# A hybrid diffusion layer on one core: the first norm's modulation as plain float32 products in four column strips, x loaded ahead of it, and three feature tiles that follow h

## The chip, the cores and the metric

The kernel runs on one core of a Trainium2 chip. The metric is device microseconds (us) for one execution of the whole layer; the number given for a kernel is the median of several runs. The engines are named as the profile names them: PE is TensorE (the matmuls, with PEld for its weight loads), DVE is VectorE, ACT is ScalarE, POOL is GpSimd, SP is SyncE, which here only starts DMAs.

## What is computed

One layer runs on 640 tokens: 128 context tokens (with the modulation of `c_ctx`) and 512 latent tokens (with that of `c`). Cut to the part that the change touches, the reference is:

```python
mod = silu(c) @ w_mod + b_mod                      # once for c_ctx, once for c; float32
sh1, sc1, g1, sh2, sc2, g2 = split(mod, 6)
h = rmsnorm(x, ng[0]) * (1.0 + sc1) + sh1          # x: 640 x 1024
z = h @ w_in                                       # zx, zg, q, k, v, g, lr, ga, gb
...                                                # RG-LRU on conv(zx), GLA on q, k, v, two gates, w_out
x = x + g1 * rmsnorm(m, ng[1])
f = square(relu(h2 @ mlp_w1)) @ mlp_w2             # h2: x under the norm with sh2, sc2
x = x + g2 * rmsnorm(f, ng[3])
```

Everything is float32. Products of the kernel reach that accuracy in two ways: plain float32 on PE, or float32r (one pass) on operands that were split into a rounded first part and a remainder, with three passes (first by first, first by remainder, remainder by first).

## The kernel before

**Recorder.** The program is first recorded in an order that is right (class `Recorder`), and then `order` hands every engine its instructions: each engine takes the oldest one whose operands are there by the estimated durations of `cost`. On the chip each engine then works through its list strictly in that order. So a list fixed by estimates decides who stands behind whom.

**Start.** SP loads x in five tiles of 128 tokens, `w_mod` in chunks of 256 columns (1 MB, four transfers of 256 KB, named `modw`), and the weights of the first products (`raw`, 1 MB for two feature tiles). `EARLY` and `MIX` (lines 48 and 49) are strings in which each letter is a step: which loads go first, and in which order the start is recorded. `x_norm` scales x by its inverse norm, `x_T` transposes it on PE into eight feature tiles `xnT`.

**Modulation of the first norm.** Eight chunks: even ones are the scale, odd ones the shift, each for two feature tiles (k tiles) of h. `mod_mm` (line 623) multiplies a chunk with the two conditioning vectors. For chunks 0 and 1 (`MOD_FULL`) it does so in plain float32 (`modw`, `cst`). For the other six it splits the chunk: ACT casts it (`modh`), DVE and POOL in turn subtract (`modl`), and PE takes both parts with the two-part vectors `csh`. The result, a row of 256 values for each request, is copied to SBUF (`rw`) and turned into columns by tiny products with `sel`; DVE makes of them the columns `a1` (scale) and `sh1` (shift).

**h.** `make_h` (line 661) scales and shifts `xnT` (128 columns on DVE, 512 on ACT), DVE casts the result to `HH` and subtracts to `HL`.

**First products.** The first unit (`first_part`, line 808) runs two feature tiles of zx, taking h's eight k tiles as they come. One feature tile is 48 matmuls of 128x320: 8 k tiles, 3 passes, 2 halves of the tokens. All later products (`fm_unit`) are one feature tile at a time, on a PSUM pool `dense` of two tiles; the pool `aux` has two more. After a tile, `post_zx` empties PSUM and does the convolution (copies `zp`, then `cv`, `xc` on ACT and DVE). Weights are split ahead (`whi` on ACT, `wlo` on DVE) into four buffers, `N_W`.

**Background.** After `first_post` (line 814) a long chain of small POOL operations, `softplus_consts` (line 683), makes the constants `n8sp` and `p4sp`. The RG-LRU chains (`xs`, gates `r` and `i`, `th`, scans) need them and run beside the products. Their gate weights `bdr` are loaded after the modulation's chunks, and ACT casts them (`bh`). GLA, the other mixer, and later modulation vectors run in the background too, and the PE goes on with products to the end of the MLP.

The lines below show how a split chunk is multiplied:

```python
copy(MOD_HI[i], hi, raw)                                          # ACT
by[MOD_LO[i]].tensor_tensor(lo, raw, f32(hi), op=OP.subtract)     # DVE or POOL
PE.matmul(out, csh[:, k, :], hi[:, kk, :], start=k == 0, stop=False)
PE.matmul(out[0:2], csh[:, k, 0:2], lo[:, kk, :], start=False, stop=k == KT - 1)
```

Of the kernel before, what the change touches and what calls it, by code (L numbers as in the profile page):

```python
# [12 lines left out]
OP = mybir.AluOpType  # L13
# [21 lines left out]
# w_mod chunks that plain float32 products take; engines (A, V, G) of the parts of the start  # L35
MOD_FULL = (0, 1)
MOD_HI, MOD_LO = "AAAA", "VGVG"
# [7 lines left out]
# the first transfers (x: a token tile, m: 256 columns of w_mod, r: rows of b_mod and norm_g), then the order in which the  # L45
# start is recorded (l: load of w_mod, X: buffers of x^T, x: transposes, m: modulation, h: two k tiles of h, p: split of
# the first weights, d: load of the next)
EARLY = "xxxmxrx"
MIX = "Xlllxlxxxxllmldmpmhmmmmhmhh"


class Op:
    """A recorded instruction."""
# [11 lines left out]
def _runs(ap, f0):  # L65
    """The runs of columns an access touches, [(lo, hi)]."""
# [20 lines left out]
def _meet(a, b):  # L87
    """Whether two accesses of a tile share a byte."""
    if a[0] >= b[1] or b[0] >= a[1]:
        return False  # L90
    ra, rb = a[2], b[2]
    if ra[0][0] >= rb[-1][1] or rb[0][0] >= ra[-1][1]:
        return False
    return any(x < d and c < y for x, y in ra for c, d in rb)
# [6 lines left out]
class Port:  # L101
    """An engine's instructions, recorded instead of issued."""
# [8 lines left out]
class Recorder:  # L111
    """Records the program in an order that is right, then issues it in an order in which no engine
    waits for an operand while another instruction could run: every engine takes the oldest
    instruction whose operands are there by the estimated times. Data hazards and the pools' slots
    (given out in the order of recording) are kept."""
# [18 lines left out]
    def cost(eng, name, args, kw, out):  # L134
        n = _dims(out)
        if eng == "PE":
            if name == "transpose":
                return max(0.05, n * 2 / 2400)
            if args[1].dtype == F32R:
                return max(n / 2400 + 0.0025, 0.106)  # L140
            return max(0.213, n * 4 / 2400)
# [22 lines left out]
    @staticmethod  # L164
    def region(ap):
        """What a hazard is looked for in: a tile of PSUM is a whole, and engines take turns at it."""
        return (0, 128, ((0, 1 << 30),)) if ap.space == bass.MemoryType.PSUM else _region(ap)
# [53 lines left out]
    def order(self):  # L221
# [24 lines left out]
        while len(out) < len(ops):  # L246
# [50 lines left out]
            if e == "PE":  # L297
                # the array runs at half its clock in a window after one that was mostly idle
# [43 lines left out]
class Piece:  # L342
    """One [128, 1024] slice of a weight, split into two float32r parts."""
# [7 lines left out]
class Load:  # L351
    """One transfer of weights into a raw buffer; n pieces are split from it."""
# [6 lines left out]
class Unit:  # L359
    """A run of matmuls on split weights and what follows it."""  # L360
# [7 lines left out]
class Stage:  # L368
    """One step of a chain: its cost (us) on VectorE and ScalarE, what it waits for, slots since the step before."""
# [5 lines left out]
class Chain:  # L375
    """Work that runs beside the large products, one stage after the other."""
# [11 lines left out]
def tile_hybrid_layer(  # L388
# [49 lines left out]
    def scaled(e, dst, src, scale, bias):  # L438
        """dst = src * scale + bias, with one of each to a partition."""
# [5 lines left out]
    # token tile 0 is the prompt; tiles 1..4 are the sample in column-major grid order  # L445
# [21 lines left out]
    # the conditioning vectors first; w_mod's shift and scale columns between the tiles of x  # L467
# [22 lines left out]
    def mod_load(m):  # L490
        """256 columns of the scale (even m) or the shift (odd m) of the first norm, two k tiles to a buffer."""
# [22 lines left out]
    # the array's clock is gated until it has been busy for a while  # L514
# [17 lines left out]
    # silu of the conditioning vectors, [128, k, (ctx, lat)]  # L532
    cst = consts.tile([128, 8, 2], F32, name="cst")
# [7 lines left out]
    # the same in two parts for each request, and what adds a request's parts up  # L541
    csh = consts.tile([128, 8, 4], F32R, name="csh")
    V.tensor_copy(csh[:, :, 0:2], cst)
    V.tensor_tensor(csh[:, :, 2:4], cst, csh[:, :, 0:2].bitcast(F32), op=OP.subtract)
    sel = consts.tile([4, 2], F32, name="sel")
    V.tensor_tensor(sel, ident[0:4, 0:2], ident[0:4, 2:4], op=OP.add)

# [1 line left out]
    w_in_r = w_in[0].rearrange("(k p) n -> p k n", p=128)  # L549

    def fm_pieces(src, n0, ncols):
        """Feature-major pieces of 128 columns, two to a transfer where there are two."""
# [12 lines left out]
    def row_pieces(src, k0):  # L565
        """Token-major pieces: one k tile by 1024 columns, two to a transfer."""
# [33 lines left out]
    junk = consts.tile([128, 512], mybir.dt.bfloat16, name="junk")  # L600

    def rstd_of(ssq, n, scale):
        """(ssq * scale + eps) ** -0.5 in place on [128, n]."""
# [4 lines left out]
    # a = norm_g * (1 + sc), sh: [128, (ctx, lat), k]  # L608
# [14 lines left out]
    def mod_mm(m):  # L623
        """256 columns of the scale (even m) or the shift (odd m) for both requests, as two columns of a1 or sh1."""
        ps = aux()
        out = ps[0:4, 0, 0:256]
        for i, raw in enumerate(modw[m]):
            if m in MOD_FULL:
                for kk in range(2):
                    PE.matmul(out[0:2], cst[:, 2 * i + kk, :], raw[:, kk, :], start=i + kk == 0, stop=2 * i + kk == KT - 1)  # L630
                continue
            hi, lo = (t_(nm, F32R)[:, 0:512].rearrange("p (k n) -> p k n", k=2) for nm in ("modh", "modl"))
            copy(MOD_HI[i], hi, raw)
            by[MOD_LO[i]].tensor_tensor(lo, raw, f32(hi), op=OP.subtract)
            for kk in range(2):
                k = 2 * i + kk
                PE.matmul(out, csh[:, k, :], hi[:, kk, :], start=k == 0, stop=False)
                PE.matmul(out[0:2], csh[:, k, 0:2], lo[:, kk, :], start=False, stop=k == KT - 1)
        rw = t_("rw")
        n = 2 if m in MOD_FULL else 4  # L640
        A.copy(rw[0:n, 0:256], out[0:n])
        for i in range(2):
            k = 2 * (m // 2) + i
            pc = ps[:, 1, 2 * i:2 * i + 2]
            PE.matmul(pc, rw[0:n, 128 * i:128 * (i + 1)], sel[0:n], start=True, stop=True)
            if m % 2:
                V.tensor_scalar(cols["sh1"][:, :, k], pc, bm(0, k), None, op0=OP.add)
            else:
                V.tensor_scalar(cols["a1"][:, :, k], pc, bm1[:, k:k + 1], ng(0, k), op0=OP.add, op1=OP.mult)
# [18 lines left out]
    # the gates' weights of two heads, [(copy, in), head, direction, (gate, out)]  # L668
# [9 lines left out]
    # softplus(-L), exactly: max(-L, 0) + 2 atanh(y / (2 + y)), y = exp(-|L|)  # L678
# [25 lines left out]
    def startup():  # L704
        do_loads(1)
# [11 lines left out]
        for s_ in MIX:  # L717
            if s_ == "l":
                modw.append(mod_load(len(modw)))
            elif s_ == "m":  # L720
                mod_mm(nm)
# [9 lines left out]
            elif s_ == "d":  # L731
                do_loads()
# [952 lines left out]
```

## Time and profile before

| what | value |
|---|---|
| three runs | 1179.06, 1180.85, 1172.89 us (median 1179.06) |
| profiled execution, span from the first to the last instruction | 1176.6 us |
| mean granted PE clock | 0.992 |
| PE busy in the span | 1146.1 us (97%) |
| DVE, ACT, POOL busy | 773.2, 571.5, 99.6 us |
| HBM read | 117.94 MB |

The profile is of one execution. Its own total is not listed apart from its span; the median of the runs lies 2.5 us above that span, which is what start and end around the first and last instruction would take if it was a median run. In the profile, a row of a timeline is one or several like instructions of an engine, with the start, the time until the last of them ended, the operation, the tile written and the tiles read, the shapes and the count; the bracket behind it is the engine's idle time just before and what released it. All helpers record through one line (L339), so tiles tell the steps apart. A plain float32 matmul stands in the trace as two records, a float32r one as one. The time to landing of a DMA counts from its issue.

### The profile page before, as it was taken

How to read it: one execution, taken by the hardware profiler on the slowest of the kernel's cores; microseconds unless marked ns; L12 is line 12 of the kernel's file. 1: busy time of each engine (PE TensorE's matmuls, PEld its weight loads, DVE VectorE, ACT ScalarE, POOL GpSimd, SP SyncE). 2: the span in 40 equal slices, each digit the busy share in tenths (PEclk: the TensorE clock that was granted, in tenths of full speed). 3: DMA queues.
4: the chain of work that ended last, by engine and by line, in shares of the span. 5: the costliest groups of instructions: out<-in, count | busy, mean ns of one | idle time of the engine just before them, and what ended most of it. 6: DMA issues, size and time to landing. Idle time of an engine off the chain costs nothing.

```text
span 1176.6 us, 17840 instructions
## 1 busy us (share of the span) xinstructions
PE 1146.1 (97%) x7188; PEld 1071.5 (91%) x7188; DVE 773.2 (66%) x1159; ACT 571.5 (49%) x911; POOL 99.6 (8%) x163
## 2 busy tenths in 40 slices
PE   7799899999999999999999999999999999999996
PEld 5599899999999999999999879999999999988995
DVE  4977966778484737629977478986455544555546
ACT  6668897995574758512342278422222222222222
POOL 3646113000000000000000021000000000000001
PEclk9999999999999999999999999999999999999998
DMA  9625336341312212227543446632322222222202
GB/s 279 217 63 153 110 84 172 77 129 55 108 59 68 72 55 72 90 89 240 174 169 134 145 139 198 214 121 72 104 76 72 72 72 72 72 73 81 94 5 89
DMA packets 101011, 130.65 MB, mean 111 GB/s; under 512 B 7790, under 2 KB 77632, under 8 KB 100928
## 3 DMA queue, kind: packets, MB, share of 16 engines
q1 hardware_dynamic: 98880, 127.61, 34.9%
q0 software_dynamic: 2048, 1.90, 0.6%
q8 instruction: 56, 0.92, 0.3%
q14 instruction: 27, 0.22, 0.1%
HBM read 117.94 MB, written 3.68 MB: 103 GB/s over the span
## 4 chain that ended last, share of the span: by engine, by line
PE 76%; DVE 8%; DMA 6%; ACT 4%; issue 3%; POOL 2%; SPq 0%; DVEq 0%; POOLq 0%; ACTq 0%
PE dense L339 62%; PE aux L339 15%; DMA modw<-in_w_mod_dram 2%; DVE i L339 2%; DMA i<-r 1%; DVE wlo L339 1%; DMA r<-r 1%; DMA raw<-in_w_in_dram 1%; DVE th L339 1%; DMA xb<-in_x_sample_dram 1%; POOL spp L339 1%; ACT r L339 1%; ACT th L339 1%; ACT whi L339 1%; DVE cv L339 1%
## 5 line engine op out<-in xcount | busy, mean ns | idle before, releaser
L339 ACT CAST whi<-raw 128x1024 fp32r<-128x1024 f32 (+1 forms) x159 | 164.2, 1037 | 392.8 <-PE dense L339 365.6
L339 DVE TENSOR_TENSOR wlo<-raw,whi 128x1024 fp32r<-128x1024 f32 x154 | 188.0, 1223 | 170.7 <-ACT whi L339 170.2
L339 PE MATMUL dense<-HH,whi 128*128 128x320 f32 x784 | 182.1, 313 | 5.6 <-DVE lrs L339 3.6
L339 PE MATMUL dense<-HL,whi 128*128 128x320 f32 x784 | 180.5, 311 | 0.6 <-DVE HL L339 0.6
L339 PE MATMUL dense<-HH,wlo 128*128 128x320 f32 x768 | 176.9, 311 | 0.0
L339 PEld LDWEIGHTS dense<-HH,whi 128*128 128x128 f32 x784 | 131.7, 189 | 7.0 <-DVE lrs L339 3.9
L339 PEld LDWEIGHTS dense<-HL,whi 128*128 128x128 f32 x784 | 132.1, 189 | 0.9 <-DVE HL L339 0.7
L339 PEld LDWEIGHTS dense<-HH,wlo 128*128 128x128 f32 x768 | 129.5, 189 | 0.2
L339 PE MATMUL dense<-H2H,whi 128*128 128x320 f32 (+2 forms) x496 | 116.8, 309 | 0.0
L339 PE MATMUL dense<-H2H,wlo 128*128 128x320 f32 (+2 forms) x496 | 116.5, 308 | 0.0
L339 PE MATMUL dense<-H2L,whi 128*128 128x320 f32 (+2 forms) x496 | 116.5, 308 | 0.0
L339 PEld LDWEIGHTS dense<-H2H,whi 128*128 128x128 f32 x496 | 84.6, 188 | 1.2
L339 PEld LDWEIGHTS dense<-H2L,whi 128*128 128x128 f32 x496 | 84.0, 188 | 0.0
L339 PEld LDWEIGHTS dense<-H2H,wlo 128*128 128x128 f32 x496 | 83.9, 188 | 0.0
L339 DVE SCALAR_TENSOR_TENSOR mac<-mw,cst,mac 128x512 f32<-128x512 f32 x112 | 77.9, 749 | 2.7 <-DMA mw<-in_w_mod_dram 2.5
L339 PE MATMUL dense<-whi,al 128*128 128x512 f32 (+1 forms) x192 | 75.2, 392 | 0.0
L339 PE MATMUL dense<-wlo,ah 128*128 128x512 f32 (+1 forms) x192 | 75.2, 392 | 0.0
L339 PE MATMUL dense<-whi,ah 128*128 128x512 f32 (+1 forms) x192 | 75.1, 391 | 0.0
L339 PE MATMUL aux<-whi,al 128*128 128x512 f32 (+1 forms) x132 | 51.6, 391 | 0.0
L339 PE MATMUL aux<-wlo,ah 128*128 128x512 f32 (+1 forms) x132 | 51.6, 391 | 0.0
L339 PE MATMUL aux<-whi,ah 128*128 128x512 f32 (+1 forms) x132 | 51.5, 390 | 0.0
L339 ACT ACT_TABLE_LOAD x36 | 46.2, 1283 | 2.5 <-DMA r<-r 1.1
(310 smaller groups left out, 2235.6 us busy)
## 6 DMA issues: line engine op xcount, KB each, us to landing
raw<-in_mlp_w_dram SPq DMA_DIRECT2D x34, 1024.0 KB, 5.4
raw<-in_w_in_dram SPq DMA_DIRECT2D x24, 1024.0 KB, 5.3
mw<-in_w_mod_dram SPq DMA_DIRECT2D x64, 256.0 KB, 5.9
modw<-in_w_mod_dram SPq DMA_DIRECT2D x32, 256.0 KB, 5.9
raw<-in_w_out_dram SPq DMA_DIRECT2D x8, 1024.0 KB, 4.9
i<-r SPq DMA_DIRECT2D x32, 160.0 KB, 3.4
raw<-in_w_in_dram SPq DMA_DIRECT2D x8, 512.0 KB, 4.3
raw<-in_lru_up_dram SPq DMA_DIRECT2D x4, 1024.0 KB, 5.3
```

The source lines that it names most:

```text
L339: getattr(eng[o.eng], o.name)(*o.args, **o.kw)
```

## The change

Three things change, all in the first part of the program.

1. The eight chunks of the first modulation all go in plain float32; nothing is split. `mod_pair` takes a scale chunk and a shift chunk together. The vectors stand in a zero-padded tile of 32 columns (`cst32`), and the eight k tiles of a chunk go in turn to four strips of 32 output partitions; k tiles 4 to 7 start a strip's sum, 0 to 3 end it. One copy brings the 128 x 512 results to SBUF, and `sel` (now 128 rows) adds the strips as it turns rows into columns. A pair is 16 recorded matmuls, and there are four pairs.
2. All of x is loaded ahead of `w_mod`, the second MB of `raw` ahead of the last four chunks; the steps of the start are recorded in another order (`MIX`), and `cost` (which only orders the lists) takes a quarter of the former time for a strip's matmul.
3. The first unit has three feature tiles in place of two (`N_FIRST`); the third has a PSUM tile of `aux`. `softplus_consts` follows the third tile's convolution in place of the second's.

```diff
-MOD_FULL = (0, 1)
-MOD_HI, MOD_LO = "AAAA", "VGVG"
-EARLY = "xxxmxrx"
-MIX = "Xlllxlxxxxllmldmpmhmmmmhmhh"
+EARLY = "xxxrxxmm"
+MIX = "XdllxxxxxDllmphllmhmhmh"
+N_FIRST = 3
...
+            if out.ap[0][1] <= 32 and n >= 128:
+                return n / 2400 + 0.0025
...
-    cst = consts.tile([128, 8, 2], F32, name="cst")
+    cst32 = consts.tile([128, 8, 32], F32, name="cst32")
+    cst = cst32[:, :, 0:2]
+    G.memset(cst32, 0.0)
...
-    csh = consts.tile([128, 8, 4], F32R, name="csh")
-    V.tensor_copy(csh[:, :, 0:2], cst)
-    V.tensor_tensor(csh[:, :, 2:4], cst, csh[:, :, 0:2].bitcast(F32), op=OP.subtract)
-    sel = consts.tile([4, 2], F32, name="sel")
-    V.tensor_tensor(sel, ident[0:4, 0:2], ident[0:4, 2:4], op=OP.add)
+    sel = consts.tile([128, 2], F32, name="sel")
+    V.tensor_tensor(sel, ident[:, 0:2], ident[:, 32:34], op=OP.add)
+    for j in (2, 3):
+        V.tensor_tensor(sel, sel, ident[:, 32 * j:32 * j + 2], op=OP.add)
...
-    def mod_mm(m):
...
+    def mod_pair(n):
+        ps = aux()
+        for m in (1, 0):
+            for r in (1, 0):
+                for j in (3, 2, 1, 0):
+                    k = 4 * r + j
+                    PE.matmul(ps[32 * j:32 * (j + 1), m, 0:256], cst32[:, k, :], modw[2 * n + m][k // 2][:, k % 2, :],
+                              start=r == 1, stop=r == 0)
         rw = t_("rw")
+        A.copy(rw[:, 0:512].rearrange("p (m c) -> p m c", m=2), ps[:, :, 0:256])
+        for m in range(2):
+            for i in range(2):
+                k = 2 * n + i
+                pc = ps[:, m, 256 + 2 * i:258 + 2 * i]
+                PE.matmul(pc, rw[:, 256 * m + 128 * i:256 * m + 128 * (i + 1)], sel, start=True, stop=True)
...
     def startup():
-        do_loads(1)
...
-            elif s_ == "d":
-                do_loads()
+            elif s_ in "dD":
+                do_loads(1 if s_ == "d" else 2)
...
-            first_ps.extend([dense(), dense()])
-        for u, p in enumerate(pzx[0:2]):
+            first_ps.extend([dense(), dense(), aux()])
+        for u, p in enumerate(pzx[0:N_FIRST]):
             fm_mm(first_ps[u], p, hh, hl, 0, T, (k,))
...
-        post_zx(first_ps[0], 0)
-        post_zx(first_ps[1], 1)
-        posted.add("zx0")
+        for u in range(N_FIRST):
+            post_zx(first_ps[u], u)
+            posted.add(f"zx{u}")
         rec.later = rec.ops[-1]
         softplus_consts()
```

The lists of the engines move at three places. A row gives the operation, the tile written and the tiles read, the shape written and the count. On PE, in the middle of the start of the kernel before, products of the first unit (`dense`) stand among the products of split chunks (`modl`, `modh`) and the turn to columns (`sel`):

```order
L339 MATMUL dense<-HL,whi 128x320
L339 MATMUL dense<-HH,wlo 128x320 x2
L339 MATMUL dense<-HL,whi 128x320 x2
L339 MATMUL dense<-HH,wlo 128x320
L339 MATMUL aux<-sel,rw 128x2
L339 MATMUL dense<-HH,wlo 128x320
L339 MATMUL dense<-HH,whi 128x320 x2
L339 MATMUL aux<-modl,csh 2x256
L339 MATMUL aux<-modh,csh 4x256
```

In the changed kernel the same engine has, from the last transposes of x on:

```order
L340 MATMUL dense<-ident,xb_101 128x128 x4
L340 MATMUL aux<-modw,cst_113 32x256 x16
L340 MATMUL aux<-sel,rw 128x2 x4
L340 MATMUL aux<-modw,cst_113 32x256 x16
L340 MATMUL dense<-HH,whi 128x320 x2
L340 MATMUL dense<-HL,whi 128x320 x2
L340 MATMUL aux<-sel,rw 128x2
L340 MATMUL dense<-HH,wlo 128x320 x2
L340 MATMUL dense<-HH,whi 128x320
```

The chunks' products moved together: all 16 of a pair in a block, and the first unit's products start behind the second pair's block. On ACT, around the last but one pair, the kernel before has:

```order
L339 ACTIVATE xnT_141<-xnT_141,sh_118,a_117 128x512
L339 ACTIVATE xnT_142<-xnT_142,sh_118,a_117 128x512
L339 CAST whi<-raw 128x1024 x2
L339 COPY rw<-aux 4x256
L339 CAST bh<-bdr 128x512
L339 ACTIVATE xnT_143<-xnT_143,sh_118,a_117 128x512
L339 ACTIVATE xnT_144<-xnT_144,sh_118,a_117 128x512
```

and the changed kernel has:

```order
L340 COPY rw<-aux 128x512
L340 ACTIVATE xnT_143<-xnT_143,sh_121,a_120 128x512
L340 ACTIVATE xnT_144<-xnT_144,sh_121,a_120 128x512
L340 CAST bh<-bdr 128x512
L340 COPY rw<-aux 128x512
L340 ACTIVATE xnT_145<-xnT_145,sh_121,a_120 128x512
L340 ACTIVATE xnT_146<-xnT_146,sh_121,a_120 128x512
```

The cast of the gate weights (`bh`) moved ahead of the copy `rw` of the last pair. Later on ACT, from the cast of the second gate weights to the `spy` that starts the softplus chain (its first operation is an absolute value, its second the exponential behind the table load), the kernel before has:

```order
L339 CAST bh<-bdr 128x512
L339 CAST xs<-xc_257 64x640 x2
L339 CAST whi<-raw 128x1024
L339 ACTIVATE spy<-C_107 128x16
L339 CAST xs<-xc_260 64x640 x2
L338 ACT_TABLE_LOAD
L339 ACTIVATE spy<-spy 128x16
L339 COPY zp<-dense 128x8x24
L339 COPY zp<-dense 128x8x40
```

and the changed kernel, from the cast of the second tile's `xs` on, has:

```order
L340 CAST xs<-xc_204 64x640 x2
L340 ACTIVATE r<-aux,C_111 128x640
L340 ACTIVATE spy<-C_111 128x16
L340 CAST bh<-bdr 128x512
L340 ACTIVATE r<-aux,C_111 128x640 x2
L340 COPY zp<-dense 128x8x24
L340 COPY zp<-dense 128x8x40
L340 ACTIVATE r<-aux,C_111 128x640
L340 ACTIVATE cv<-zp,C_111 128x656
L340 CAST whi<-raw 128x8x32 x3
L339 ACT_TABLE_LOAD
L340 ACTIVATE spy<-spy 128x16
```

The exponential moved behind the first gates (`r`), another convolution (`cv`) and the three casts of the low-rank weights (`whi` of 128x8x32).

## Rows read from the trace of the kernel before

**Rows 1.** Page, busy tenths in 40 equal slices of the span: PE.

```profile
PE   7799899999999999999999999999999999999996
```

**Rows 2.** Busy time by stretch: us, each engine's busy us (records), PE clock, DMA share, GB/s.

```profile
0.00:28.50 28.50, 22.62 (x125) 15.45 (x125) 13.09 (x48) 17.87 (x53) 9.44 (x25) 0.94 0.96 276
...
0.00:44.00 44.00, 34.65 (x205) 23.52 (x206) 27.85 (x70) 27.58 (x72) 19.25 (x33) 0.96 1.00 302
...
55.00:60.00 5.00, 5.00 (x23) 3.41 (x22) 3.35 (x8) 2.57 (x5) 0.00 (x0) 0.50 0.00 0
...
79.00:100.00 21.00, 21.00 (x145) 21.00 (x144) 17.60 (x26) 18.91 (x31) 17.25 (x35) 1.00 0.48 120
100.00:150.00 50.00, 46.18 (x310) 45.66 (x309) 42.82 (x62) 42.08 (x55) 12.11 (x25) 0.97 0.42 120
150.00:300.00 150.00, 147.41 (x1078) 146.48 (x1077) 106.54 (x153) 122.06 (x154) 13.93 (x24) 1.00 0.39 103
```

**Rows 3.** Timeline of SP's DMA queue in the start.

```profile
13.89 23.66 SPq L339 DMA_DIRECT2D modw<-in_w_mod_dram  x28
37.87 0.37 SPq L339 DMA_DIRECT2D raw<-in_w_in_dram  x1
38.59 3.53 SPq L339 DMA_DIRECT2D bdr<-in_lru_wa_dram  x4
42.16 4.56 SPq L339 DMA_DIRECT2D bdr<-in_lru_wx_dram  x4
```

**Rows 4.** The chain that ended last, around 40 us: start, us, what.

```profile
37.87 7.42 DMA raw<-in_w_in_dram
```

**Rows 5.** Groups of instructions from 0 to 70 us: busy us, mean ns | idle before.

```profile
L339 POOL TENSOR_TENSOR modl<-modw,modh 128x512 fp32r<-128x512 f32 x12 | 18.8, 1583 | 13.8 <-ACT modh L339 10.1 <-DVE xnT L339 2.6 <-PE aux L339 1.1
L339 DVE TENSOR_TENSOR modl<-modw,modh 128x512 fp32r<-128x512 f32 x12 | 14.7, 1241 | 0.2 <-issue 0.2
L339 ACT CAST modh<-modw 128x512 fp32r<-128x512 f32 x24 | 13.2, 614 | 0.3 <-DVE wlo L339 0.3
```

**Rows 6.** Tile modw, its readers on PE: ns min/median/max, first and last start.

```profile
L339 PEld LDWEIGHTS aux<-modw,cst x32: 80/85/129, 17.8 to 28.6; 128*2 128x2 f32 x32
L339 PE MATMUL aux<-modw,cst x32: 377/379/634, 17.8 to 28.8; 128*2 128x256 f32 x32
```

**Rows 7.** Timeline of PE: plain float32 chunk, first unit, and the 144th dense matmul.

```profile
24.32 2.75 PE L339 MATMUL aux<-modw,cst 128*2 128x256 f32 x12
...
52.33 0.38 PE L339 MATMUL aux<-sel,rw 4*128 4x2 f32 x2 [2.38 <-DVE sh L339]
52.63 0.41 PE L339 MATMUL dense<-HH,whi 128*128 128x320 f32 x1
...
78.22 0.46 PE L339 MATMUL dense<-HL,whi 128*128 128x320 f32 x2
78.51 0.46 PE L339 MATMUL dense<-HH,wlo 128*128 128x320 f32 x2
```

**Rows 8.** Timeline of DVE: from the modulation's columns to one k tile of h.

```profile
56.33 0.28 DVE L339 TENSOR_SCALAR a<-aux,bm,C 128x2 f32<-128x2 f32 x1 [1.24 <-PE aux L339]
56.52 0.48 DVE L339 CAST HH<-xnT 128x640 fp32r<-128x640 f32 x1
57.04 0.82 DVE L339 TENSOR_TENSOR HL<-xnT,HH 128x640 fp32r<-128x640 f32 x1
```

**Rows 9.** Timeline of ACT: gate weights' cast, h's scaling, the softplus exponential, the wait for p4sp.

```profile
59.99 0.62 ACT L339 CAST bh<-bdr 128x512 fp32r<-128x512 f32 x1
63.69 0.82 ACT L339 ACTIVATE xnT<-xnT,sh,a 128x512 f32<-128x512 f32 x1 [3.08 <-DVE sh L339]
...
82.68 0.22 ACT L339 ACTIVATE spy<-spy 128x16 f32<-128x16 f32 x1
...
102.48 2.27 ACT L339 ACTIVATE th<-r,p4sp 128x640 f32<-128x640 f32 x3 [2.41 <-POOL p4sp L339]
```

**Rows 10.** Waits of PE behind 80 us: us in total, times, longest.

```profile
PE dense L339 <- DVE lrs L339: 3.6, 1, 3.6
```

More of the change, by code (lines that the diff above doesn't have):

```diff
@@ L621, in x_norm @@
             scaled(e, x[:, 0:512], x[:, 0:512], q, None)
-    def mod_mm(m):
+    def mod_pair(n):
         ps = aux()
[L626 to L638, printed above, removed]
-        rw = t_("rw")
[L640 to L649, printed above, removed]
+        for m in (1, 0):
[4 more added lines that the diff above has]
+                              start=r == 1, stop=r == 0)
+        rw = t_("rw")
+        A.copy(rw[:, 0:512].rearrange("p (m c) -> p m c", m=2), ps[:, :, 0:256])
[4 more added lines that the diff above has]
+                PE.matmul(pc, rw[:, 256 * m + 128 * i:256 * m + 128 * (i + 1)], sel, start=True, stop=True)
+                if m:
+                    V.tensor_scalar(cols["sh1"][:, :, k], pc, bm(0, k), None, op0=OP.add)
+                else:
+                    V.tensor_scalar(cols["a1"][:, :, k], pc, bm1[:, k:k + 1], ng(0, k), op0=OP.add, op1=OP.mult)
     xnT = []
@@ L720, in startup @@
             elif s_ == "m":
-                mod_mm(nm)
+                mod_pair(nm)
                 nm += 1
@@ L820, in first_post @@
         rec.later = None
-    units.append(Unit(pzx[0:2], [lambda k=k: first_part(k) for k in range(KT)], first_post, "zx1", us=12.8, dve=12.0,
-                      act=12.0))
-    for f in range(2, KT):
+    units.append(Unit(pzx[0:N_FIRST], [lambda k=k: first_part(k) for k in range(KT)], first_post, "zx1", us=6.4 * N_FIRST,
+                      dve=6.0 * N_FIRST, act=6.0 * N_FIRST))
+    for f in range(N_FIRST, KT):
         fm_unit(pzx[f], lambda ps, f=f: post_zx(ps, f), tag=f"zx{f}", dve=2.9, act=1.7)
```

## The prediction

> **What bounds the kernel now.** I read the page's slices first: PE is nearly full from the third slice on, and the first two, some 59 us, show 7 tenths [rows 1]. So the time is the PE's work plus what the start wastes, and the change is worth what it takes out of the start. The busy times by stretch say the same: PE was busy for 147.4 of the 150 us from 150 to 300, and for 46.2 of the 50 us before [rows 2]. Then I looked for the point from which both kernels have the same PE work ahead. That is the end of the third feature tile of zx: 144 dense matmuls are done, no gate product has run. In the kernel before this is at 78.51 + 0.46 = 79.0 us [rows 7]. I call this point E. What E moves, the whole kernel moves, if nothing behind it gets in the way.
>
> Next, what sets E. Three things compete. DMA: up to the second raw the queue brings x (2.62 MB), eight chunks (8.39 MB) and two raws (2.10 MB), 13.1 MB; the last of it, the raw, landed at 37.87 + 7.42 = 45.3 [rows 3, 4]. Splitting: ACT casts 24 quarters of chunks in 13.2 us, DVE and POOL subtract them in 14.7 and 18.8 us [rows 5], and the chunks' columns come only behind that: at 52.33 PE had idled 2.38 us for a shift column, long after the last chunk had landed [rows 7]. PE: after that idle its granted clock was 0.50, the lower of its two levels, from 55 to 60 [rows 2]. So the splits are what is late, not the transfers.
>
> **What the change removes.** All 24 casts and 24 subtractions go, and the small operations on the two-part vectors with them. With them goes what delayed h on DVE between 30 and 55 us; what is late next is the transfers and then PE's own list.
>
> **The transfers.** SP's queue moves the same 13.1 MB, in another order, so its end stays at 45.3, now for the last chunk. Two chunks, the first raw and two chunks (with x, 7.86 MB) must have landed for the second pair; the mean of 276 GB/s over 28.5 us makes that 28.5 [rows 2]. The third pair needs all but the last 2.10 MB; at 302 GB/s over 44 us the whole takes 43.4, so this is between 37 and 39.5, and I take 39. The gate weights' eight transfers (8.1 us of issue, [rows 3]) stay behind the last chunk.
>
> **A pair's products.** A pair is 16 matmuls in strips, 32 records in the trace's way of counting. In the kernel before 12 such records took 2.75 us, the last one 0.38 by itself [rows 6, 7], so one follows the other by (2.75 - 0.38) / 11 = 0.215. No row shows strips side by side. The ends are 8 x 0.215 = 1.7 us (four strips together) and 32 x 0.215 = 6.9 us (one after the other). I take 16 x 0.215 = 3.4 us: both records of a matmul use the same strip, the records start in order, so the second record of a strip can run beside the first of the next strip, but no more than two at a time. While PE waits for the second pair it idles, and the clock was at its lower level after an idle of 2.4 us [rows 2, 7]; for that pair I add 1.7 us, between 0 and 3.4.
>
> **PE's list, step by step.** One dense matmul follows another by (78.51 - 78.22) / 2 = 0.147 us, one turn to columns costs 52.63 - 52.33 = 0.30 [rows 7]. By the lists, 24 dense matmuls and four turns stand between the second and third pairs (3.5 + 1.2 = 4.7), two more dense ones between the third and fourth (5.0), and 94 of the 144 and four turns behind the fourth (13.8 + 1.2 = 15.0). That gives:
>
> - second pair from 28.5 to 33.6 (3.4 + 1.7), dense to 38.3
> - third pair from 39.0 (its transfer) to 42.4, dense to 47.4
> - fourth pair, landed at 45.3, from 47.4 to 50.8
> - the rest to 65.8: E
>
> E moves by 79.0 - 65.8 = 13.2 us. The first pair's products, its columns and the first weights' split lie in the wait for the second pair's transfer.
>
> **What I cost at nothing, and its cover.** The last pair's columns pass one copy (at most the 0.82 us that a scaling of 512 columns takes, [rows 9]), turns, column (0.28), scaling (0.82), HH (0.48) and HL (0.82) [rows 8, 9], about 4.5 us. Meanwhile PE has the third tile's first four k tiles (22 matmuls) and k tiles 4 and 5 of all three (36), 8.5 us. The added wait of ACT is here: the cast of the gate weights, 0.62 us [rows 9], now stands ahead of that copy, and behind it wait the copy, h's last scaling and, through them, PE. Those weights are issued by about 48. If they land up to 4 us after the copy is due at 50.8, the cover of 8.5 against 4.5 us just holds; if later, each us costs one. The memset and the two additions for the wider vectors are done while x is still on its way.
>
> **Behind E.** One more tile must leave PSUM at once, and two of its weights' splits move behind E, some 5 us of ACT and 8 of DVE by the list. From 79 to 150 us ACT was busy 61.0 and DVE 60.4 of 71 [rows 2], so there is room for it, barely. The stall of 3.6 us on lrs in that stretch [rows 10] came from DVE's list; it may go, or up to 5 us of new waits may come. I count 0, and keep -3.6 and +5 as ends.
>
> **Sum.** Profiled execution: 1176.6 - 13.2 = 1163.4 us of span. The median of the runs lies 2.5 us above the span, so 1165.9 us. A measurement of this kernel can tell about 1% (11.8 us) from no change, so 1167.3 is the border of "faster", and the forecast lies just past it.
>
> **Rivals.** *Four strips together.* A pair takes 1.7 us. Then the transfers are the bound: fourth pair from 45.7 to 47.4, E at 62.4, gain 16.6, 1162.5 us. For it: strips write apart, and narrow weight loads of 85 ns [rows 6] hide. Against it: the two records of a matmul share a strip.
>
> *The strips don't run side by side*, so the change doesn't do what it says. A pair takes 6.9 us and PE's list is the bound: 28.5 + 3 x 6.9 + 4.7 + 5.0 + 15.0 = 73.9, gain 5.1, 1174.0 us. For it: no row shows two products in the array at once. If besides each of the 32 weight loads waits for the product ahead of it, 32 x 85 ns = 2.7 us more a pair, E is at 82.0 and the kernel is slower: 1182.1 us; this decides from 8.6 us a pair on (53.2 + 3p = 79). Against it: in the stretch at 24.32 the loads hid behind the products. The Trainium skill, "TensorE: Matmul & The Clock Gate", section "Part 3: Packing small matmuls — row/col tiling", says that weight loads overlap running matmuls only when their row groups differ, and all strips here use the same rows; by that rule the time would be this 1182.1. The same section measures 2.38 times for three column strips, which by an estimate from that page would make a pair 2.9 us. No run here shows either yet.
>
> *The background is the bound.* The softplus chain now starts behind the third tile, and its exponential on ACT behind the casts of the low-rank weights, which need a buffer that the fifth tile's weights hold. So it comes after two more tiles (2 x 48 x 0.147 = 14.1) and 16 gate products (2.4), and some ACT steps, about E + 19 = 85, against 82.68 before. From there to p4sp took 102.48 - 82.68 = 19.8 us [rows 9], so th starts at 104.6, 2.1 us later than before, though PE is 13 us ahead. If the RG-LRU chain from there on, and not PE, sets the next 200 us, all of the gain is lost, and the kernel is 2.1 us slower: 1181.2. For it: ACT waited 2.41 us for p4sp [rows 9]. Against it: PE idled only 6.4 us from 100 to 300 [rows 2], and the results of that chain are needed late.
>
> **How the numbers follow.** Forecast 0.46, with its own range of 1161.5 to 1171 (clock, landing, new waits); four strips together 0.22; one after the other 0.16, and with waiting loads 0.05; background 0.11. Below 1167.3 lie six tenths of the forecast and nearly all of the second case, 0.50. Past 1190.9 only several of the bad ends together would lead, 0.03. The rest, 0.47, is within 1%. The range of 1159.5 to 1176 leaves out the two slower cases and the tail of a gain with the lrs stall gone as well.
>
> **What would show it.** Right: no modh or modl; the last chunk lands near 45; the blocks of 32 records last about 3.4 us at the full clock; the 144th dense matmul ends near 66; E's gain still stands at the end. Wrong: blocks of 7 us or more; an idle PE behind the fourth pair, for a column or for HL; PE waits in 100 to 300 that add up to far more than 6.4 us, with th or p4sp as the releaser.

## The result, and the profile after

| kernel | median us | before, same chip | ratio, 95% interval |
|---|---|---|---|
| changed | 1161.66 | 1177.65 | 0.9865 [0.9836, 0.9893] |
| changed, on another chip | 1163.63 | 1177.80 | 0.9882 [0.9861, 0.9902] |

So the change takes 14 to 16 us, 1.2 to 1.4%. The forecast was 1165.9 us (range 1159.5 to 1176), by its case of two strips at a time; the time that came is that of the rival *four strips together*, 1162.5. In the profiled execution the span fell by 1176.6 - 1158.9 = 17.7 us. One run of e9 below took 2257.28 us; its median and its ratio are those of its five other runs.

The page's slices of the changed kernel, to be held against [rows 1]: the first slice is still not full, the second, 7 tenths before, now is.

```profile
PE   6999999999999999999999999999999999999996
```

Busy time by stretch, the columns of [rows 2]. PE is at its lower level around the second pair, from about 28 to 34 (and from about 17 to 20, as in the kernel before); from 55 to 60, where it was at 0.50 before, it runs at 1.00. From 100 to 300 its idle time is 2.7 + 2.8 = 5.5 us, against 6.4 before.

```profile
30.00:32.00 2.00, 2.00 (x24) 0.96 (x20) 1.22 (x2) 0.00 (x0) 0.00 (x0) 0.50 1.09 348
32.00:34.00 2.00, 2.00 (x15) 1.09 (x8) 0.39 (x1) 1.47 (x3) 0.00 (x0) 0.50 1.10 349
...
55.00:60.00 5.00, 5.00 (x36) 5.00 (x35) 0.69 (x1) 0.62 (x1) 1.87 (x4) 1.00 0.03 9
...
100.00:150.00 50.00, 47.32 (x346) 46.89 (x345) 35.98 (x50) 48.83 (x61) 9.37 (x16) 1.00 0.42 114
150.00:300.00 150.00, 147.22 (x1052) 145.25 (x1051) 110.51 (x163) 118.56 (x157) 10.53 (x17) 1.00 0.38 106
```

The timeline of PE: the second pair's block, the first dense matmul, the third and fourth blocks with the row that follows each, a turn to columns between dense matmuls, and the last product of the third tile, which is E.

```profile
29.54 3.64 PE L340 MATMUL aux<-modw,cst 128*32 128x256 f32 x32 [1.34 <-DMA modw<-in_w_mod_dram]
33.11 0.90 PE L340 MATMUL dense<-HH,whi 128*128 128x320 f32 x2
...
38.55 1.93 PE L340 MATMUL aux<-modw,cst 128*32 128x256 f32 x32
40.41 0.56 PE L340 MATMUL dense<-HH,whi 128*128 128x320 f32 x2
...
42.21 0.46 PE L340 MATMUL dense<-HH,wlo 128*128 128x320 f32 x2
42.50 0.28 PE L340 MATMUL aux<-sel,rw 128*128 128x2 f32 x2
42.64 0.54 PE L340 MATMUL dense<-HH,whi 128*128 128x320 f32 x2
43.02 0.46 PE L340 MATMUL dense<-HL,whi 128*128 128x320 f32 x2
...
45.16 1.93 PE L340 MATMUL aux<-modw,cst 128*32 128x256 f32 x32
47.03 0.56 PE L340 MATMUL aux<-HL,whi 128*128 128x320 f32 x2
...
61.95 0.46 PE L340 MATMUL aux<-HH,wlo 128*128 128x320 f32 x2
```

E is 61.95 + 0.46 = 62.4 in place of 79.0 [rows 7]: 16.6 of the 17.7 us. A block of 32 records takes 40.41 - 38.55 = 1.86 us from its start to the next instruction's, 0.06 a record, where one record took 0.215 before. No bracket stands behind the third and fourth blocks: from 29.54 on PE never waits until E. A turn takes 43.02 - 42.21 - 4 x 0.147 = 0.22 us of PE's list. Taken the same way, a turn of the kernel before took 63.72 - 62.63 - 4 x 0.147 = 0.50 us (lines below); the 0.30 of the prediction is only the time from its start to the next start.

```profile
62.63 0.45 PE L339 MATMUL dense<-HH,wlo 128*128 128x320 f32 x2
63.02 0.38 PE L339 MATMUL aux<-sel,rw 4*128 4x2 f32 x2
63.33 0.56 PE L339 MATMUL dense<-HH,whi 128*128 128x320 f32 x2
63.72 0.46 PE L339 MATMUL dense<-HL,whi 128*128 128x320 f32 x2
```

The tile `modw`, its readers on PE (columns of [rows 6]): a record lasts as long as before, so it is not short, it lies beside others; the 32 weight loads of a block, at 106 ns or more each, come to 3.4 us and fit into 1.86.

```profile
L340 PEld LDWEIGHTS aux<-modw,cst x128: 106/110/178, 20.6 to 46.5; 128*32 128x32 f32 x128
L340 PE MATMUL aux<-modw,cst x128: 376/379/636, 20.6 to 46.7; 128*32 128x256 f32 x128
```

Waits of PE behind E (us in total, times, longest). The 3.6 for `lrs` [rows 10] are gone; these two are now the longest:

```profile
PE aux L340 <- ACT r L340: 2.9, 3, 1.7
PE aux L340 <- DVE xs L340: 1.7, 1, 1.7
```

ACT and POOL: the last pair's copy behind the gate weights' cast, the softplus exponential, `p4sp` and `th`, to be held against [rows 9]. `th` starts 1.1 us earlier than before, and no longer waits for `p4sp`.

```profile
46.95 0.62 ACT L340 CAST bh<-bdr 128x512 fp32r<-128x512 f32 x1 [1.24 <-DMA bdr<-in_lru_wx_dram]
47.48 0.58 ACT L340 COPY rw<-aux 128x512 f32<-128x512 f32 x1
...
80.91 0.22 ACT L340 ACTIVATE spy<-spy 128x16 f32<-128x16 f32 x1
...
101.38 2.99 ACT L340 ACTIVATE th<-r,p4sp 128x640 f32<-128x640 f32 x4
```

```profile
99.19 0.75 POOL L340 TENSOR_SCALAR p4sp<-spp 128x16 f32<-128x16 f32 x1
```

### The profile page after: what moved, and what is told of

It reads as the page before. It is cut to its first block, busy times and chain, and to the rows that moved or that the text cites. A ratio compares the mean times of both kernels' runs of the same rounds, so it can differ in the third digit from the quotient of the medians.

```text
span 1158.9 us, 17719 instructions
## 1 busy us (share of the span) xinstructions
PE 1131.3 (98%) x7188; PEld 1064.3 (92%) x7188; DVE 755.6 (65%) x1147; ACT 557.8 (48%) x882; POOL 80.1 (7%) x152
## 4 chain that ended last, share of the span: by engine, by line
PE 78%; DVE 8%; ACT 5%; DMA 5%; issue 2%; POOL 1%; SPq 0%; DVEq 0%; POOLq 0%; ACTq 0%
PE dense L340 62%; PE aux L340 16%; DVE i L340 2%; DVE th L340 2%; DMA i<-r 1%; DVE wlo L340 1%; DMA modw<-in_w_mod_dram 1%; ACT L340 1%; ACT r L340 1%; ACT th L340 1%; DMA raw<-in_w_in_dram 1%; DMA w2raw<-in_gla_w_dram 1%; DMA r<-r 1%; ACT whi L340 1%; ACT L339 0%
## 5 line engine op out<-in xcount | busy, mean ns | idle before, releaser
L340 PE MATMUL dense<-HH,whi 128*128 128x320 f32 x768 | 178.1, 312 | 0.2 <-ACT vc L340 0.2
L340 PE MATMUL dense<-HL,whi 128*128 128x320 f32 x768 | 176.1, 310 | 0.0
L340 PE MATMUL dense<-HH,wlo 128*128 128x320 f32 x752 | 172.4, 309 | 0.0
L340 PEld LDWEIGHTS dense<-HH,whi 128*128 128x128 f32 x768 | 128.4, 188 | 2.1 <-issue 0.8
L340 PEld LDWEIGHTS dense<-HL,whi 128*128 128x128 f32 x768 | 128.9, 188 | 0.0
L340 PEld LDWEIGHTS dense<-HH,wlo 128*128 128x128 f32 x752 | 125.9, 188 | 0.0
L340 PE MATMUL dense<-whi,HH 128*128 128x256 f32 x160 | 45.0, 281 | 0.0
```

What stands on the lines that cost most here:

```text
L340: getattr(eng[o.eng], o.name)(*o.args, **o.kw)
```

## The experiments

Theory: the strips run side by side, PE's list behind the second pair's landing sets E, and the time follows E. Rivals: the loads' order or the third tile carry the gain; the transfers set E; the softplus chain or other waits behind E take part of it. Three kernels change the strips, three put one part alone into the kernel before, two undo a part, one moves softplus, two try to gain more, and one is the change again.

| run | E | span | span - E | median us | ratio, 95% interval |
|---|---|---|---|---|---|
| before | 79.0 | 1176.6 | 1097.6 | 1177.65 | 1 |
| changed | 62.4 | 1158.9 | 1096.5 | 1161.66 | 0.9865 [0.9836, 0.9893] |
| changed again (e10) | 63.0 | 1162.8 | 1099.8 | 1163.63 | 0.9882 [0.9861, 0.9902] |
| e4 plain, no strips | 79.7 | 1178.5 | 1098.8 | 1178.09 | 0.9997 [0.9985, 1.0010] |
| e11 strips alone | 65.1 | 1158.0 | 1092.9 | 1160.42 | 0.9847 [0.9829, 0.9866] |
| e12 third tile alone | 77.7 | 1175.4 | 1097.7 | 1175.86 | 0.9978 [0.9962, 0.9994] |
| e1 one strip | 82.6 | 1182.8 | 1100.2 | 1183.63 | 1.0038 [1.0023, 1.0053] |
| e2 two strips | 69.7 | 1169.6 | 1099.9 | 1171.12 | 0.9934 [0.9909, 0.9958] |
| e6 two wide strips | 67.4 | 1165.6 | 1098.2 | 1166.64 | 0.9902 [0.9879, 0.9925] |
| e3 two tiles | 64.7 | 1163.3 | 1098.6 | 1164.98 | 0.9885 [0.9859, 0.9910] |
| e8 loads as before | 63.4 | 1162.3 | 1098.9 | 1165.55 | 0.9886 [0.9865, 0.9907] |
| e5 softplus earlier | 63.3 | 1164.0 | 1100.7 | 1165.10 | 0.9881 [0.9861, 0.9901] |
| e7 idle products | 66.8 | 1163.7 | 1096.9 | 1165.63 | 0.9886 [0.9866, 0.9905] |
| e9 start reordered | 60.9 | 1159.1 | 1098.2 | 1162.52 | 0.9873 [0.9850, 0.9896] |

E is the end of the third tile's last product (of the 144th dense matmul where that tile comes behind the first two). Chips differ by up to 2 us in the kernel before (1177.65 to 1179.47), so ratios are what is compared.

**e1, e2, e6: how many strips run side by side.** (`raw` is the k tile's part of `modw`, `s` is k % 2.)

```diff
-    PE.matmul(ps[32 * j:32 * (j + 1), m, 0:256], cst32[:, k, :], raw, start=r == 1, stop=r == 0)
+    PE.matmul(ps[0:32, m, 0:256], cst32[:, k, :], raw, start=k == 7, stop=k == 0)                            # e1
+    PE.matmul(ps[32 * s:32 * (s + 1), m, 0:256], cst32[:, k, :], raw, start=k > 5, stop=k < 2)               # e2
+    PE.matmul(ps[64 * s:64 * (s + 1), m, 0:256], cst32[:, 2 * k:2 * k + 64], raw, start=k > 5, stop=k < 2)   # e6
```

> All eight k tiles of a chunk go to the first strip of 32 partitions, one after the other; the engines' lists are those of the changed kernel, only the copy rw takes 32 partitions. Theory (the strips run side by side, and the time follows E, the end of the 144th dense matmul): a block of 32 records at the full clock takes 6.9 us (32 x 0.215) in place of 1.93; behind the second pair's landing PE's list is full, so three blocks add 3 x 5.0 = 14.9 us, less up to 1.7 us because the second block may no longer find the lower clock: E at 75.5 to 77.5, and 1174.5 to 1177 us in place of 1161.7. Rival (a record is short because its weights are 32 columns wide and not because strips run side by side): the block stays near 1.9 us and the time at 1161.7. Rival (the transfers, not PE's list, set E): blocks of 6.9 us, but E at most 68 and a time under 1168.

> k tiles go in turn to two strips; lists as in the changed kernel, the copy rw takes 64 partitions. Theory (as many records run side by side as there are strips in turn): a block takes 32 x 0.215 / 2 = 3.4 us at the full clock, three blocks add 3 x 1.5 = 4.5 us: E at 66 to 67, time 1165.5 to 1167. Rival (the two records of a matmul share a strip, so that what overlaps is the second record of one strip and the first of the next): two strips are as good as four, block 1.9 us, time 1161.7. Rival (time does not follow E): block 3.4 us, time within 1.5 us of 1161.7.

> Two strips again, but 64 partitions wide, so that all 128 rows of rw are written and a turn to columns multiplies 128 rows with sel, where e2's had 64. (Of a strip's 64 rows only the first two hold a result; the rest meets zeros in sel.) In e2 a turn took 0.50 us out of PE's list, in the changed kernel 0.22 to 0.26; 12 turns behind 29.5. Theory (products with fewer than 128 rows cost the list more, and this is what E in e2 had beyond the blocks): blocks of 3.65 (second one 5.07), E at 62.4 + 1.4 + 2 x 1.7 = 67.2, within 0.7; time 1166 to 1168.5, against 1171.1 in e2. Rival (the rows of a turn don't matter): E at 69.5 to 70.2, time 1170 to 1172.

On PE's timeline, the third block of e1, then that of e2 with a turn of 64 rows, then a turn of 128 rows in e6:

```profile
46.48 7.09 PE L340 MATMUL aux<-modw,cst 128*32 128x256 f32 x32
53.50 0.56 PE L340 MATMUL dense<-HH,whi 128*128 128x320 f32 x2
```

```profile
40.46 3.65 PE L340 MATMUL aux<-modw,cst 128*32 128x256 f32 x32
44.04 0.56 PE L340 MATMUL dense<-HH,whi 128*128 128x320 f32 x2
...
56.97 0.31 PE L340 MATMUL dense<-HH,wlo 128*128 128x320 f32 x1
57.21 0.38 PE L340 MATMUL aux<-sel,rw 64*128 64x2 f32 x2
57.52 0.56 PE L340 MATMUL aux<-HH,whi 128*128 128x320 f32 x2
57.92 0.46 PE L340 MATMUL aux<-HL,whi 128*128 128x320 f32 x2
```

```profile
55.16 0.30 PE L340 MATMUL dense<-HH,wlo 128*128 128x320 f32 x1
55.30 0.28 PE L340 MATMUL aux<-sel,rw 128*128 128x2 f32 x2
55.44 0.54 PE L340 MATMUL aux<-HH,whi 128*128 128x320 f32 x2
55.82 0.45 PE L340 MATMUL aux<-HL,whi 128*128 128x320 f32 x2
```

Start to next start, a block takes 7.02 us in one strip, 3.58 in two, 1.86 in four: 1 to 1.96 to 3.77. The theory holds. The rival that two strips do as well as four falls, and with e1, whose weights are 32 columns wide too, the rival that these make a record short; that e1's E is past 68 answers the rival that the transfers set it. My sizes of E for e1 and e2 were too small, though, and with them the times: 82.6 against 75.5 to 77.5, 69.7 against 66 to 67. In e1 the first block counts too: it delays the second from 29.54 to 31.04, and the second pays 9.77 - 7.09 = 2.7 us for the lower clock, where the changed kernel's pays 1.7. In both a turn costs more: in e2 it takes 57.92 - 56.97 - 3 x 0.147 = 0.51 us, in e6, with 128 rows, 55.82 - 55.16 - 3 x 0.147 = 0.22. e6 is e2 with turns of 128 rows, by strips twice as wide: E falls from 69.7 to 67.4, where 67.2 was expected, and the ratio from 0.9934 to 0.9902, with intervals that overlap. As turns cost 0.50 in the kernel before too, some 2 of the 16.6 us that the change gains in E are, by an estimate from e2 and e6, the cheaper turns and not the strips. E sets the time: e1's is 20.2 us later than the changed kernel's, and its ratio is 0.0173 higher, which is 20.4 us. Steps of a few us in E can't be told in the time: e7's E lies 3.8 us behind e10's, at ratios of 0.9886 and 0.9882.

**e4, e11, e12: one part alone, put into the kernel before.** e4 takes every chunk in plain float32; e11 does so in strips; e12 has only the third tile.

```diff
-MOD_FULL = (0, 1)
+MOD_FULL = (0, 1, 2, 3, 4, 5, 6, 7)                                                                          # e4
...
+        for k in range(KT):                                                                                  # e11
+            j = k % 4
+            PE.matmul(ps[32 * j:32 * (j + 1), 0, 0:256], cst32[:, k, :], modw[m][k // 2][:, k % 2, :], start=k < 4, stop=k > 3)
...
-        for u, p in enumerate(pzx[0:2]):
+        for u, p in enumerate(pzx[0:3]):                                                                     # e12
```

> The kernel before with all eight chunks in plain float32, two columns of weights, no strips, and the order of loads, steps and tiles as before. Theory (without the splits PE's own list is the bound): eight chunks of 16 records take 8 x 3.4 = 27.5 us of PE, 144 dense matmuls 21.2, 16 turns 4.8; from the first chunk at 17.8 this gives E at 71.3 with no idle time, 72 to 76 with some: time 1171 to 1175 against 1177.7 before. Rival (the splits cost nothing that counts): 1177.7 or more, since PE has 10 us more work. Rival (the splits were the whole loss, strips add nothing): 1161 to 1165.

> The kernel before with one part of the change alone: every chunk in plain float32 in four strips, by itself (8 matmuls, a copy, two turns); the order of loads and steps and the two tiles of the first unit stay as before. The lists now mix the strips' matmuls in twos and threes with dense ones. Theory (the strips are nearly the whole change; loads' order and third tile are worth 2 to 3 us of E together): last chunk lands near 44, its columns and h's last two k tiles take 4 us more, then 24 dense matmuls of two tiles (3.5) and the third tile (7.1): E at 60 to 66, time 1163 to 1167 where the kernel before has 1178. Rival (strips that alternate with dense matmuls no longer run side by side; then a record costs 0.2 us again and the modulation 15 us or more of PE): E at 68 to 73, time 1169 to 1174. Rival (the order of the loads or the third tile is what lets the strips count): time 1174 or more.

> The kernel before with the other part alone: three feature tiles in the first unit, softplus constants behind the third; split products and loads as before. Theory (PE waits for the splits' columns at most 2.4 us at a time in the kernel before, and the third tile can fill only that and what its lower clock costs): E at 75.5 to 78.5 in place of 79.0, time 1174.5 to 1178. Rival (the third tile is worth as much as the whole change): 1166 or less. Rival (its splits delay the chunks' splits on ACT and DVE): E past 79, time over 1179.

e4's ratio is 0.9997: taking the splits away gains nothing by itself. That is the first rival's case, and not the theory's (E at 72 to 76, 1171 to 1175 us); its sum had 0.30 for each of 16 turns, which take 0.5 here too. The PE timeline shows why nothing is gained: the list, made by estimates, puts all chunks ahead of h, and the first dense matmul comes at 56.50, and from 28.5 to 62 us PE is never idle.

```profile
55.54 1.02 PE L339 MATMUL aux<-modw,cst 128*2 128x256 f32 x4
56.50 0.56 PE L339 MATMUL dense<-HH,whi 128*128 128x320 f32 x2
```

e11 (the strips, with the turns of 128 rows that belong to them) has all of the gain: 0.9847, not slower than the whole change, and 1160.4 us, under the 1163 to 1167 expected. Its E is 2 to 3 us later than the changed kernel's, as expected for the missing parts and short of the 68 to 73 of the rival that strips between dense matmuls lose all their gain; its time behind E is 4 to 7 us shorter. The waits of PE behind 62 us add up to 5.4 us in e11, against 7.7 and 9.7 in the two profiles of the changed kernel; the greatest in e11 and in e10:

```profile
PE aux L341 <- DVE la L341: 1.6, 1, 1.6
...
PE aux L341 <- ACT r L341: 0.3, 1, 0.3
```

```profile
PE aux L340 <- ACT r L340: 4.9, 3, 2.7
```

e12 gains 0.2%, E 1.3 us: the first theory.

**e3, e8: one part taken out of the changed kernel.**

```diff
-N_FIRST = 3
+N_FIRST = 2               # e3
...
-EARLY = "xxxrxxmm"
+EARLY = "xxxmxrxm"        # e8
```

> The changed kernel with two feature tiles in the first unit in place of three; the softplus constants then follow the second tile. Theory (the third tile only fills what PE would wait for the last pair's columns): h's last k tiles come at about 51; by then PE has from 29.5 on three blocks (7.5), 72 dense matmuls (10.6) and turns (3.0), so it idles some 1 to 3 us, part of it at the lower clock: E 1 to 4 us later than 62.4, time 1162.5 to 1166. Rival (the third tile is worth most of the gain): PE idles for the 36 to 44 matmuls that are missing, 5.3 us or more, time 1167 or more. Rival (worth nothing or negative because of the later softplus constants and the PSUM tile it takes): time 1161.7 or less.

> The changed kernel with the first chunk of w_mod loaded between the third and the fourth tile of x, as before. Theory (the first pair's block waits for the transposes of x, and there are about 3 us of slack up to the second pair's landing): x's last tile lands 2.9 us later, the first block starts 2 to 3 us later than 20.6, its turns end near 30.5, the second block starts 0 to 1.5 us later: E at 62.4 to 64.2, time 1161.5 to 1164. Rival (x first is worth a part of the gain as large as the third tile's): E 3 us later or more, time 1165 or more.

E of both is where the theory has it. e8's time is past the 1164 expected, on a chip where the kernel before is slower too (1179.47). But 0.9885 and 0.9886 can't be told from the change itself (0.9865 and 0.9882): neither part is worth anything that these runs can show.

**e10: the changed kernel again.** Its profile shows how far one execution of the same kernel lies from another.

> The changed kernel as it is, once more, on the chip of the run beside it: its E and its time on this chip are the measure for the other runs, whose starts came 0.7 to 0.9 us later in their traces than in its first one. All theories: a ratio to before of 0.984 to 0.989 and an E of 62.4 to 63.4, by when the second pair lands (29.5 to 30.4).

As expected. The list is the same, E comes 0.6 us later, and the time behind E is 3.3 us longer. So one profile's span is good to some 4 us, and the 17.7 us above are the upper end.

**e5: softplus constants behind the second tile.**

```diff
             posted.add(f"zx{u}")
-        rec.later = rec.ops[-1]
-        softplus_consts()
+            if u == 1:
+                rec.later = rec.ops[-1]
+                softplus_consts()
```

> The changed kernel with the softplus constants recorded behind the second feature tile's convolution, as before, and not behind the third's. The exponential then runs some 10 us earlier than at 80.9. Theory (the chain of p4sp and th is late but nothing on PE's path waits for it): E stays at 62.4, p4sp some 5 to 10 us earlier, time 1160.5 to 1163 (1161.7 in the changed kernel). Rival (the later chain costs part of the gain by its waits for r and xs, 4.6 us behind E): those waits go, time 1157 to 1159.5.

`p4sp` ended at 92.5 in place of 99.9, and the ratio is 0.9881: nothing gained (1165.1 us is past the theory's range, on a chip where the kernel before is slower too). PE's waits behind E changed their names (a 1.8 us wait for `zp` came), not their sum (9.0 us, between the 7.7 and 9.7 of the changed kernel). The rival falls.

**e7: PE kept busy ahead of the second pair.**

```diff
+            PE.matmul(ahead[0][:, 1, 384:512], ident, ident, start=True, stop=True)    # 11, 3, 1, 1 and 6 times
```

> The changed kernel with 22 idle products of the identity in the gaps of PE between the first and the second pair (11 ahead of the turns, 5 between them, 6 behind), into an unused part of the second pair's PSUM tile. Theory A (behind the second pair's landing PE's list sets E, so what the lower clock costs counts): the second block takes 1.93 us at 1.00 in place of 3.64 at 0.50, and E comes 1.5 to 2 us earlier, at 60.4 to 60.9, with no idle PE ahead of the third block; time about 1160. Theory B (the third and fourth pair's transfers are just as late): PE waits for the third pair near 38.2, and E gains 0 to 0.8 us; time 1161 to 1161.7. Rival (the clock is not held by such products): second block still at 0.50 and 3.6 us.

Neither theory. The second block did run in 1.93 us at 1.00, but the list of ACT came out with both casts of the second `raw` ahead of the second pair's copy. The transfer of `raw`, then two casts, then the copy: PE waited 2.53 us, and its granted clock was 0.50 until past 40. E came 4.4 us later than in the first profile of the changed kernel. ACT and PE of e7, and the clock:

```profile
33.68 1.99 ACT L341 CAST whi<-raw 128x1024 fp32r<-128x1024 f32 x2 [3.07 <-DMA raw<-in_w_in_dram]
35.57 0.58 ACT L341 COPY rw<-aux 128x512 f32<-128x512 f32 x1
```

```profile
30.81 1.93 PE L341 MATMUL aux<-modw,cst 128*32 128x256 f32 x32
...
36.20 0.59 PE L341 MATMUL aux<-sel,rw 128*128 128x2 f32 x2 [2.53 <-ACT rw L341]
```

```profile
31.00:32.00 1.00, 1.00 (x24) 0.61 (x20) 0.96 (x3) 0.00 (x0) 0.00 (x0) 1.00 1.09 349
...
38.00:40.00 2.00, 2.00 (x10) 2.00 (x9) 0.28 (x1) 0.00 (x0) 0.00 (x0) 0.50 1.10 368
```

**e9: the start reordered by what e7 showed.**

```diff
-MIX = "XdllxxxxxDllmphllmhmhmh"
+MIX = "XdllxxxxxDllmhpllmPhmhmh"
...
+            rec.ahead, rec.later = SPLIT_AHEAD, hi_after     # the cast whi goes behind the pair's rw
+            A.copy(hv, src)
+            rec.later = lo_after                             # wlo behind the first HL, or the columns
+            V.tensor_tensor(lv, src, f32(hv), op=OP.subtract)
...
+                if nm == 2:
+                    third.append(aux())
+                    PE.matmul(third[0][:, 1, 400:402], ident, ident[:, 0:2], start=True, stop=True)
```

> The changed kernel with its start reordered by what e7 showed: the first two weight splits follow the first pair's copy rw and the next two the second pair's (their subtractions behind the first tile's HL and the second pair's columns), a pair's four turns go ahead of the four columns, and the third feature tile's PSUM tile is given out ahead of the third pair's, so that its products can fill PE while the third pair's transfer is on its way. Theory (E is set by what PE has to do behind the second pair's landing, and by the third pair's landing near 38.2): 8 dense matmuls move ahead of the second block, the first dense starts near 27 in place of 33.1, PE waits 1 to 2 us for the third pair, E at 59.5 to 61, some 2 us earlier; time 1 to 3 us under that of the changed kernel run beside it. Rival (as with the idle products of e7, a wait elsewhere takes it all back): E at 62.4 or later, time the same or more. Rival (the waits for r and xs behind E grow by what E gains): E earlier, time the same.

The first dense matmul starts at 26.87 and E is 60.9, 2.1 us earlier than in e10 on the same chip, as the theory has it, though the wait for the third pair that it expected didn't come. Of the time 1.1 us is seen, and 0.9873 [0.9850, 0.9896] against 0.9882 [0.9861, 0.9902] tells nothing. No run here is shown to beat the change.

## Why the prediction was right, and where it was off

- *What bounds the kernel; E.* Right. In all runs but e11 (1092.9) the time behind E lies between 1096.5 and 1100.7 us, while E goes from 60.9 to 82.6.
- *The splits are what is late.* Only half the truth. e4 shows that behind them PE's own list is just as late: E at 79.7 without any split. That the splits go counts only together with products that cost PE a quarter of plain ones (1.86 us a pair, against 32 x 0.215 = 6.9).
- *Transfers.* Close. The second pair landed at 29.54 (taken: 28.5), the third by 38.55 (39), the last by 45.16 (45.3).
- *A pair's products, "I take 16 x 0.215 = 3.4 us ... no more than two at a time".* This is the step that failed, a term mis-sized. 3.4 is what two strips take (3.58 in e2); four take 1.86. That both records of a matmul use one strip did not hold them to two at a time: in the first 0.22 us of the third block four records run in the changed kernel, two in e2, one in e1 (rows below, in this order; the number in brackets counts them). The clock's term was right: 1.7 us added for the second pair, 3.64 - 1.93 = 1.71 measured.

```profile
38.54:38.76 0.22, 0.21 (x4) 1.00 1.09 349
40.46:40.68 0.22, 0.22 (x2) 1.00 1.08 345
46.47:46.69 0.22, 0.21 (x1) 1.00 0.67 102
```

- *PE's list.* 0.147 for a dense matmul held; a turn took 0.22 in place of 0.30. With 1.9 us for a block and 0.08 less for a turn, the same list gives 39.0 + 1.9 + 4.7 + 1.9 + 14.7 = 62.2, and 62.4 was measured. That the third block started near those 39.0, at 38.55, is partly luck: the second pair landed 1.0 us later than taken, its block was 1.5 us shorter (3.57 against 5.1), and the dense matmuls and turns behind it took 5.4 us against 4.7, the first of them still at the lower clock.
- *One after the other.* The rival did not come, but e1 is its case: 1183.6, near the 1182.1 of its bound by luck, and not for the reason given there: the weight loads hid in e1 as well (7.02 / 32 = 0.219 a record, against 0.215). Without exposed loads the rival's sum is 1174.0; most of the rest is the second block, later by 2.5 us and longer by 2.8, and the turns. The Trainium skill's rule ("TensorE: Matmul & The Clock Gate", "Part 3: Packing small matmuls — row/col tiling") that loads overlap running matmuls only when their row groups differ did not hold in these runs: all strips use the same rows, and a block's loads, 3.4 us, fit into its 1.86. The same section's 2.38 times for three column strips lies between the 1.96 for two and 3.77 for four here, lower for each strip (0.79 against 0.98 and 0.94).
- *The last columns' cover.* Held. ACT waited 1.24 us for `bdr`, the copy started at 47.48, 0.4 us behind the block's end, and PE did not wait.
- *The background.* The exponential came at E + 18.5 (forecast E + 19), `p4sp` 19.0 us behind it (19.8). That it would bind PE was wrong, as forecast; e5 shows that moving it earlier gains nothing.
- *Behind E: 0, between -3.6 and +5.* The first profile has -1.1 us against before, the second +2.2. The ends were right. Why e11 has some 5 us less there than the others is open: its waits for `r` are down to 0.3 us, but its lists differ from the changed kernel's in too much to name one cause.
- *Sum.* 1165.9 against 1161.7 and 1163.6: 2 to 4 us too slow. Two blocks at 1.5 us too much make 3.0 of the 3.4 us by which E was forecast too late, and the turns the rest. And a run's time lies 1.75 us above its span (1160.65 and 1158.9), not the 2.5 that was added.

## What to carry to other kernels

Where a product has few output columns (two here), try sending its k tiles to separate 32-column strips, with the strips added up in the step that follows: here, in plain float32, this divided the time of a block by 1.96 with two strips and by 3.77 with four. Before splitting operands for a faster pass, look whether plain products in strips are fast enough; the casts and subtractions then fall away. And measure the parts of a change alone: here one of three had the whole gain, and a move of 2 us in the start could not be told from the time behind it, which differed by 3 us between two profiles of one kernel.

## What the runs showed that was not expected

- A product with fewer than 128 rows between full ones costs PE's list more, with the same output of two columns: a turn of 2 rows 0.51 us (e4), of 4 rows 0.50 (the kernel before), of 64 rows 0.51 (e2), of 128 rows 0.22 (e6 and the changed kernel).
- Strips that alternate with full products lose most of their gain. In e11 two matmuls (four records) between dense ones take 44.15 - 43.11 - 2 x 0.147 = 0.75 us of PE's list, where four records of a whole block take 1.86 / 8 = 0.23. Two matmuls fill only two strips, and two strips take 3.58 / 8 = 0.45 for four records, so 0.2 us of the loss is that; 0.3 us comes on top.

```profile
43.11 0.31 PE L341 MATMUL dense<-HL,whi 128*128 128x320 f32 x1
43.35 0.63 PE L341 MATMUL aux<-modw,cst 128*32 128x256 f32 x4
43.90 0.41 PE L341 MATMUL dense<-HL,whi 128*128 128x320 f32 x1
44.15 0.31 PE L341 MATMUL dense<-HH,wlo 128*128 128x320 f32 x1
```

Both are changes between products that use the whole array and products that use a part of it. The Trainium skill ("TensorEngine Tiling (Array Packing)", "Key Properties") says that a change of the tiling mode drains the engine. The 0.3 us more in either case (0.51 - 0.22, 0.75 - 0.45) agree with it; no run here separates the drain from other causes.

- In e7 PE had no gap between the first and the second block, because idle products filled them, and its granted clock was 1.00 in the second block. In the changed kernel it idled five times there, 5.3 us in all, and the clock was 0.50 in that block.
